# Forgetting attention: the reciprocals of the denominators multiply the head's result, as a row brought through DRAM, and v's remainders are made in one VectorE operation a block

## The chip, the cores and the metric

The kernel runs on one core of one Trainium2 chip. The metric is the device time of one execution in microseconds. Five engines work side by side, each through its own queue in order: TensorE (PE in the profile, its weight loads PEld), VectorE (DVE), ScalarE (ACT), GpSimd (POOL) and SyncE (SP), which here issues nearly all DMAs. The five meet through semaphores.

## The reference

One layer of a hybrid model in float32, for 512 tokens of width 1024: a feed-forward block, a mixing block with two branches (a chunked mLSTM and a forgetting attention), and a second feed-forward block, each with modulated normalisation and a residual. The change lies in the forgetting attention, 16 heads of width 64:

```python
def forgetting_attention(q, k, v, f_pre, q_g, k_g):
    ...
    F = jnp.moveaxis(jnp.cumsum(jax.nn.log_sigmoid(f_pre.astype(f32)), axis=1), 1, 2)
    ...
        logits = jnp.einsum('bhqd,bhkd->bhqk', q_blk, k).astype(f32) * scale + (F_blk[..., :, None] - F[..., None, :])
        logits = jnp.where(k_pos[None, :] <= q_pos[:, None], logits, -jnp.inf)
        p = jax.nn.softmax(logits, axis=-1)
        return jnp.einsum('bhqk,bhkd->bhqd', p.astype(v.dtype), v)
```

softmax divides each row of exponentials by its sum. The division may be made on the probabilities, before the product with v, or on that product, since the sum depends on the query alone.

## The kernel before

**Precision.** Every float32 product is made of rounded parts: an operand is split into a high part (the value as the matmul rounds it) and its remainder. `split` (L81) does it for weights: `raw` is loaded by SP (L78, three buffers), `wh` copied by ScalarE (L88), `wl` subtracted by VectorE (L89, four buffers each). `mm3` (L104) makes three matmuls of the four parts.

**The mixing stage.** After the gates and the mLSTM, `run` (L966 to L985) goes through 18 steps n. Step n calls `fox_s(n)`, `fox_o(n - 2)` and `fox_p(n - 1)`; between them stand pieces of a generator `fill`, which has the projections: `fox_qkv(g + 1)` makes q, k and v of the next group of four heads (chunks of weights, four token blocks each), and beside the last group `y_a` makes the mLSTM branch's output gate. `fox_t` makes the transposed q and k of a pair of heads.

**One head.** `fox_s` (L745): a row of decays `A0` is brought from DRAM (`A_d`) to all partitions by SP and masked by POOL into `Am` (L753). For each of four query blocks two matmuls (L761, L762) make logits in PSUM, VectorE adds the decays and takes the minimum of the negated logits (L764, L768, into `mn`), and ScalarE exponentiates (L772), with the sum of each row into `sm` (128 partitions x 4 blocks). `fox_p` (L775), one step later: the reciprocal of `sm` (L779), then four products on VectorE that scale the blocks of `S` (L782, 128 to 512 columns). Ten transposes on TensorE (L790) turn the blocks so that keys lie on partitions; each bank is split into `Ph` (ScalarE, L788) and its remainder `Pl` (VectorE, L789). `fox_o` (L806), one step after that: eight matmuls (L820) of `vt` with `Ph` and `Pl`. `vt` has the high part of v in 64 columns and its remainder in the next 64, so the two halves of the PSUM bank `po` are added: ScalarE copies one half to `tmp` (L823), VectorE adds the other and writes 64 rows of `yb` (L824).

**v.** In `fox_qkv`, `donev` (L697) adds the bias (VectorE, L699), and for each of two pairs of heads ScalarE copies the high part (L702) and POOL subtracts the remainder (L703), 128 columns each. POOL also scales q and k by their norms (L694), with the factors that VectorE's `rsqrt` made (L133 last).

**Order.** The kernel's text gives priorities and dependencies. The order in which each engine's queue has its instructions is made by the framework's scheduler when the kernel is built, from its own costs. On the chip each queue then keeps that order, and an instruction whose semaphore isn't there holds all behind it. PSUM has two pools of four banks, `pg` for projections (tile g) and `pt` for the rest (tile t). `yb` lies in the eight buffers that held x until it was stored to `x_d`; it is read only when the second branch is made (L999).

Of the kernel before, what the change touches and what calls it, by code (L numbers as in the profile page):

```python
# [11 lines left out]
F32 = mybir.dt.float32  # L12
F32R = mybir.dt.float32r
I32 = mybir.dt.int32
AF = mybir.ActivationFunctionType
# [5 lines left out]
P = 128  # L21
T = 512
NT = 4
# [18 lines left out]
P_OFF = (0, 128, 384, 768)  # L42
PT_OFF = (0, 768, 1152, 512)
MUL, ADD, SUB, MAX, MIN = ALU.mult, ALU.add, ALU.subtract, ALU.max, ALU.min


class Layer:
# [534 lines left out]
    def v_mlstm(self, half, ap, ip):  # L582
        nc, w = self.nc, self.A["w_mix"][0]
        bb = self.bias_bcast([(VM + half * 512, 512)], ip)
        vt = []
        for i in range(2):
            pair = [ap.tile([P, NT, 258], F32R, name=self.nm("vm"), tag="vm", bufs=6) for _ in range(2)]
            nc.scalar.activation(pair[0][:, :, 256:258], self.onz, AF.Copy)
            nc.scalar.activation(pair[1][:, :, 256:258], self.onz, AF.Copy, scale=0.0)
            vt.append(pair)  # L590
        def done(tb, ps):
            f = self.tmp(ip, "vf")
            nc.vector.tensor_tensor(f, ps, bb, op=ADD)
            for i in range(2):
                hi, lo = vt[i]
                s = slice(i * 256, (i + 1) * 256)
                nc.scalar.activation(hi[:, tb, 0:256], f[:, s], AF.Copy)
                nc.vector.tensor_tensor(lo[:, tb, 0:256], f[:, s], hi[:, tb, 0:256], op=SUB)
        def mk(ch):
            def make():  # L600
                wh, wl = self.w_mov(w, ch * 256, VM + half * 512)
                return wh, wl, 2 * ch, 2
            return make
        self.vt[2 * half:2 * half + 2] = vt
        yield from self.u_gemm_tokens([mk(c) for c in range(4)], 512, done)
# [60 lines left out]
    def fox_qkv(self, g, ip):  # L666

        nc, sp, w = self.nc, self.sp, self.A["w_mix"][0]
        o = g * 256
        bb = self.bias_bcast([(QF + o, 256), (KF + o, 256)], ip)  # L670
        tok = [ip.tile([P, 512], F32, name=self.nm("tk"), tag="tok", bufs=4) for _ in range(NT)]
        ss = sp.tile([P, NT, 8], F32, name=self.nm("fs"), tag="fs", bufs=2)
        def done(tb, ps):
            nc.vector.tensor_tensor(tok[tb], ps, bb, op=ADD)
            j = self.tmp(ip, "fj")
            nc.scalar.activation(j, tok[tb], AF.Square)
            nc.vector.tensor_reduce(ss[:, tb, :], j.rearrange("p (h d) -> p h d", h=8), AX.X, ADD)
        def mk(ch):
            def make():
                sh = [P, 2, 512]  # L680
                rows = w[ch * 256:(ch + 1) * 256]
                r = self.raw(sh, [(lambda t, i=i: t[:, :, i * 256:(i + 1) * 256],
                                   rows[:, c + o:c + o + 256].rearrange("(k p) n -> p k n", p=P))
                                  for i, c in enumerate((QF, KF))])
                wh, wl = self.split(r, sh)
                return wh, wl, 2 * ch, 2
            return make
        yield from self.u_gemm_tokens([mk(c) for c in range(4)], 512, done)
        v = sp.tile([P, NT * 8], F32, name=self.nm("fv"), tag="fv", bufs=2)
        nc.vector.tensor_scalar(v, ss.rearrange("p b h -> p (b h)"), 1.0 / 64, EPS, op0=MUL, op1=ADD)  # L690
        r = self.rsqrt(v, NT * 8)
        for tb in range(NT):
            t3 = tok[tb].rearrange("p (h d) -> p h d", h=8)
            nc.gpsimd.tensor_tensor(t3, t3, r[:, tb * 8:(tb + 1) * 8].unsqueeze(2).to_broadcast([P, 8, 64]), op=MUL)  # L694
        bv = self.bias_bcast([(VF + o, 256)], ip)
        vt = [ip.tile([P, NT, 2, P], F32R, name=self.nm("fvt"), tag="vm", bufs=6) for _ in range(2)]
        def donev(tb, ps):  # L697
            f = ip.tile([P, 256], F32, name=self.nm("vg"), tag="t2", bufs=3)
            nc.vector.tensor_tensor(f, ps[:, :256], bv[:, :256], op=ADD)  # L699
            for pr in range(2):  # L700
                f2 = f[:, pr * P:(pr + 1) * P].rearrange("p (h d) -> p h d", h=2)
                nc.scalar.activation(vt[pr][:, tb, :, 0:64], f2, AF.Copy)  # L702
                nc.gpsimd.tensor_tensor(vt[pr][:, tb, :, 64:P], f2, vt[pr][:, tb, :, 0:64], op=SUB)  # L703
        def mkv(ch):
            def make():
                sh = [P, 4, 256]
                r = self.raw(sh, [(lambda t: t, w[ch * 512:(ch + 1) * 512, VF + o:VF + o + 256]
                                   .rearrange("(k p) n -> p k n", p=P))])
                wh, wl = self.split(r, sh)
                return wh, wl, 4 * ch, 4  # L710
            return make
        self.fx[g] = (tok, vt)
        yield from self.u_gemm_tokens([mkv(c) for c in range(2)], 256, donev)
# [31 lines left out]
    def fox_s(self, h, ip):  # L745

        nc, sp = self.nc, self.sp
# [9 lines left out]
        for qb in range(NT):  # L757
# [12 lines left out]
                m = mn[:, qb, 1:2]  # L770
            ws = slice(o, o + (qb + 1) * P)
            nc.scalar.activation(S[:, ws], S[:, ws], AF.Exp, scale=-1.0, bias=m, accum_out=sm[:, qb:qb + 1])  # L772
        self.S[h] = (S, sm)

    def fox_p(self, h, ip):  # L775

        nc = self.nc
        S, sm = self.S[h]
        nc.vector.reciprocal(sm, sm)  # L779
        for qb in range(NT):  # L780
            ws = slice(P_OFF[qb], P_OFF[qb] + (qb + 1) * P)
            nc.vector.tensor_scalar(S[:, ws], S[:, ws], sm[:, qb:qb + 1], None, op0=MUL)  # L782
        Ph = ip.tile([P, 1408], F32R, name=self.nm("Ph"), tag="p6", bufs=5)
        Pl = ip.tile([P, 1408], F32R, name=self.nm("Pl"), tag="p6", bufs=5)
        nc.scalar.activation(Ph[:, 512:640], self.ident, AF.Copy, scale=0.0)
# [20 lines left out]
    def fox_o(self, h, ip):  # L806

        nc = self.nc
        g, i = h // 4, h % 4
        pr, hb = i // 2, (i % 2) * 64  # L810
        rows = slice(hb, hb + 64)
        vt = self.fx[g][1]
        Ph, Pl = self.S[h]
        po = self.tbank()
        blk = ((0, 0, 0), (1, 768, P), (2, 1152, 256), (3, 512, 256))
        n = 0
        for kb, o, q0 in blk:
            for Px in (Ph, Pl):
                n += 1
                nc.tensor.matmul(po[:, q0:], vt[pr][:, kb, i % 2, :], Px[:, o:o + T - q0], start=n == 1, stop=n == 8)  # L820
        tmp = self.tmp(ip, "yt")
        ot = slice(64 - hb, 128 - hb)
        nc.scalar.activation(tmp[rows, :], po[ot, :], AF.Copy)  # L823
        nc.vector.tensor_tensor(self.yb[2 * g + pr][rows, :], po[rows, :], tmp[rows, :], op=ADD)  # L824


    def y_a(self, m, ap, ip):
# [45 lines left out]
    def run(self):  # L873
        nc, tc, A = self.nc, self.tc, self.A
        gain = lambda r: self.colA[:, r:r + NK]
        self.x_d = self.dp.tile([T, D], F32, name="x_d")
        self.h_d = self.dp.tile([T, D], F32, name="h_d")

        self.ntmp, self.xn_tiles = 5, self.xn_start
        with tc.tile_pool(name="f1t", bufs=1) as tp:  # L880
# [175 lines left out]
```

## Time and profile before

| | |
|---|---|
| median of 3 runs | 1382.25 us |
| lowest, highest | 1380.84, 1384.68 us |
| the profiled execution | 1384.43 us |
| its span in the profile | 1382.7 us |
| mean granted TensorE clock | 0.993 |
| instructions | 17469 |
| DMA, mean over the span | 127 GB/s |

The page gives busy time by engine, the chain of work that ended last and the costliest groups. A busy TensorE is not one at its peak, and the engines' shares are means over stages that differ: the mixing stage's attention lies between 560 and 800 us. There, windows (busy time of each engine in a stretch), the timeline (instructions in order of time, with the idle time before one and what ended it, in brackets) and the waits (who waited for whom, total, times, longest) say more than the page. In a group's row stand the line, the engine, the operation, result and operands, the shapes and the count, then total and mean time, then the engine's idle time before such an instruction.

### The profile page before, as it was taken

How to read it: one execution, taken by the hardware profiler on the slowest of the kernel's cores; microseconds unless marked ns; L12 is line 12 of the kernel's file. 1: busy time of each engine (PE TensorE's matmuls, PEld its weight loads, DVE VectorE, ACT ScalarE, POOL GpSimd, SP SyncE). 2: the span in 40 equal slices, each digit the busy share in tenths (PEclk: the TensorE clock that was granted, in tenths of full speed). 3: DMA queues.
4: the chain of work that ended last, by engine and by line, in shares of the span. 5: the costliest groups of instructions: out<-in, count | busy, mean ns of one | idle time of the engine just before them, and what ended most of it. 6: DMA issues, size and time to landing. Idle time of an engine off the chain costs nothing.

```text
span 1382.7 us, 17469 instructions
## 1 busy us (share of the span) xinstructions
PE 1349.1 (98%) x6570; PEld 1128.7 (82%) x6570; DVE 797.0 (58%) x1439; ACT 554.4 (40%) x940; POOL 131.0 (9%) x151
## 2 busy tenths in 40 slices
PE   6999999999999999999999999999999999999998
PEld 5788887887888888788787888888888888888887
DVE  7865666656467788888798542444473333332232
ACT  4442333323237654667567542422353232232120
POOL 4200000000011101331431100011010000000000
PEclk9999999999999999999999999999999999999999
DMA  9665556665533433432334233533313333333330
GB/s 290 193 204 178 183 183 206 212 207 194 178 80 107 131 92 110 130 92 78 95 82 119 69 99 101 159 92 106 107 53 116 106 92 96 103 92 96 110 122 31
DMA packets 212392, 176.02 MB, mean 127 GB/s; under 512 B 10386, under 2 KB 182066, under 8 KB 212308
## 3 DMA queue, kind: packets, MB, share of 16 engines
q1 hardware_dynamic: 211828, 174.83, 42.0%
q8 instruction: 52, 0.85, 0.3%
q14 instruction: 32, 0.26, 0.1%
q0 software_dynamic: 416, 0.06, 0.0%
q10 hardware_dynamic: 64, 0.02, 0.0%
HBM read 168.51 MB, written 6.36 MB: 126 GB/s over the span
## 4 chain that ended last, share of the span: by engine, by line
PE 84%; DVE 9%; ACT 3%; issue 2%; SPq 1%; DMA 1%; POOL 1%; DVEq 0%; ACTq 0%; POOLq 0%
PE g L108 22%; PE g L106 22%; PE g L107 22%; PE t L106 4%; PE t L108 4%; PE t L107 4%; DVE wl L89 2%; PE t L820 1%; PE t L790 1%; ACT wh L88 1%; DMA ar<-in_w_ada_dram 1%; DVE ac L444 1%; PE t L761 1%; DVE S L782 1%; PE t L762 1%
## 5 line engine op out<-in xcount | busy, mean ns | idle before, releaser
L89 DVE TENSOR_TENSOR wl<-raw,wh 128x1024 fp32r<-128x1024 f32 x214 | 273.6, 1279 | 309.2 <-ACT wh L88 289.8
L88 ACT ACTIVATE wh<-raw 128x1024 fp32r<-128x1024 f32 (+1 forms) x221 | 231.7, 1053 | 516.7 <-PE g L107 192.4
L108 PE MATMUL g<-uh,wl 128*128 128x512 f32 (+2 forms) x984 | 369.8, 377 | 1.7 <-DVE wl L89 1.7
L106 PE MATMUL g<-uh,wh 128*128 128x512 f32 (+2 forms) x984 | 370.9, 378 | 0.0
L107 PE MATMUL g<-ul,wh 128*128 128x512 f32 (+2 forms) x984 | 370.3, 377 | 0.0
L108 PEld LDWEIGHTS g<-uh,wl 128*128 128x128 f32 (+1 forms) x984 | 185.0, 188 | 36.4 <-DVE wl L89 2.6
L106 PEld LDWEIGHTS g<-uh,wh 128*128 128x128 f32 (+1 forms) x984 | 185.2, 188 | 34.1 <-ACT wh L88 0.6
L107 PEld LDWEIGHTS g<-ul,wh 128*128 128x128 f32 (+1 forms) x984 | 185.3, 188 | 33.6
L106 PE MATMUL g<-wh,uh 128*128 128x512 f32 (+1 forms) x320 | 113.4, 354 | 0.0
L107 PE MATMUL g<-wl,uh 128*128 128x512 f32 (+1 forms) x320 | 112.2, 351 | 0.0
L108 PE MATMUL g<-wh,ul 128*128 128x512 f32 (+1 forms) x320 | 112.1, 350 | 0.0
L325 DVE TENSOR_TENSOR sl<-g,sl 128x512 f32<-128x512 f32 (+1 forms) x45 | 30.0, 666 | 86.7 <-PE g L108 86.5
L284 DVE SCALAR_TENSOR_TENSOR acc<-raw,ccol,acc 128x1024 f32<-128x1024 f32 x49 | 62.8, 1282 | 16.2 <-DMA raw<-in_w_ada_dram 15.6
L106 PE MATMUL g<-wh,hh 128*128 128x512 f32 x176 | 69.3, 394 | 0.0
L108 PE MATMUL g<-wh,hl 128*128 128x512 f32 x176 | 69.2, 393 | 0.0
L106 PE MATMUL t<-wh,hh 128*128 128x512 f32 x176 | 69.1, 393 | 0.0
L107 PE MATMUL t<-wl,hh 128*128 128x512 f32 x176 | 69.1, 392 | 0.0
L107 PE MATMUL g<-wl,hh 128*128 128x512 f32 x176 | 69.1, 392 | 0.0
L108 PE MATMUL t<-wh,hl 128*128 128x512 f32 x176 | 69.1, 392 | 0.0
L108 PEld LDWEIGHTS g<-wh,ul 128*128 128x128 f32 x320 | 61.0, 191 | 7.8
L106 PEld LDWEIGHTS g<-wh,uh 128*128 128x128 f32 x320 | 61.2, 191 | 7.1
L107 PEld LDWEIGHTS g<-wl,uh 128*128 128x128 f32 x320 | 61.2, 191 | 7.0
(264 smaller groups left out, 1930.0 us busy)
## 6 DMA issues: line engine op xcount, KB each, us to landing
raw<-in_ffn_w_in_dram SPq DMA_DIRECT2D x82, 512.0 KB, 4.0
raw<-in_w_ada_dram SPq DMA_DIRECT2D x56, 512.0 KB, 3.4
raw<-in_w_mix_dram SPq DMA_DIRECT2D x48, 512.0 KB, 4.1
raw<-in_ffn_w_out_dram SPq DMA_DIRECT2D x44, 512.0 KB, 4.2
raw<-in_w_mix_dram SPq DMA_DIRECT2D x32, 256.0 KB, 2.9
ar<-in_w_ada_dram SPq DMA_DIRECT2D x28, 256.0 KB, 6.0
A<-A_d SPq DMA_DIRECT2D x16, 256.0 KB, 4.0
raw<-in_w_branch_a_dram SPq DMA_DIRECT2D x8, 512.0 KB, 4.2
```

Of the source, the lines that this page charges most:

```text
L88: nc.scalar.activation(hi, src, AF.Copy)
L89: (eng or nc.vector).tensor_tensor(lo, src, hi, op=SUB)
L106: mm(ps, lh, rh, start=start, stop=False)
L107: mm(ps, lh, rl, start=False, stop=False)
L108: self.last_mm = mm(ps, ll, rh, start=False, stop=stop)
L284: nc.vector.scalar_tensor_tensor(acc, r, self.ccol[:, k:k + 1], acc, op0=MUL, op1=ADD)
L325: nc.vector.tensor_tensor(s[:, :w], ps_b[:, c0:c1], s[:, :w], op=MUL)
L444: nc.vector.scalar_tensor_tensor(a, r[:, i], cc, a, op0=MUL, op1=ADD)
L761: nc.tensor.matmul(ps[:, :w], q[:, s], k[:, :w], start=True, stop=False)
L762: nc.tensor.matmul(ps[:, :w], q[:, s], kl[:, :w], start=False, stop=True)
L782: nc.vector.tensor_scalar(S[:, ws], S[:, ws], sm[:, qb:qb + 1], None, op0=MUL)
L790: tr = lambda b, c, qb, kb: nc.tensor.transpose(b[:, c:c + P], S[:, P_OFF[qb] + kb * P:P_OFF[qb] + (kb + 1) * P], self.ident)
```

## The change

Four things are changed.

- The scaling of `S` in `fox_p` is left out; `Ph` and `Pl` hold exponentials that are not normalised.
- The reciprocal of `sm` is made at the end of `fox_s`. Two DMAs on SP follow it: one writes the 128 x 4 reciprocals to a DRAM tile of the head, `r_d[h]`, as a row of 512 in the order of the tokens; the other reads that row into 64 partitions of `yb`, where the head's result will stand.
- `fox_o` adds the halves into `tmp` and then multiplies `tmp` with what stands in `yb`, in one more VectorE operation of 64 x 512.
- `vt` is one tile for four heads instead of two for a pair each, so that ScalarE copies the 256 columns of a block in one operation; the remainders are made by one VectorE operation instead of two on POOL. The mLSTM's v tiles, which share the buffers, are allocated in pairs accordingly.

```diff
--- before.py
+++ after.py
@@ -584,7 +584,8 @@
         bb = self.bias_bcast([(VM + half * 512, 512)], ip)
         vt = []
         for i in range(2):
-            pair = [ap.tile([P, NT, 258], F32R, name=self.nm("vm"), tag="vm", bufs=6) for _ in range(2)]
+            t = ap.tile([P, 2, NT, 258], F32R, name=self.nm("vm"), tag="vm", bufs=3)
+            pair = t[:, 0], t[:, 1]
             nc.scalar.activation(pair[0][:, :, 256:258], self.onz, AF.Copy)
             nc.scalar.activation(pair[1][:, :, 256:258], self.onz, AF.Copy, scale=0.0)
             vt.append(pair)
@@ -693,14 +694,13 @@
             t3 = tok[tb].rearrange("p (h d) -> p h d", h=8)
             nc.gpsimd.tensor_tensor(t3, t3, r[:, tb * 8:(tb + 1) * 8].unsqueeze(2).to_broadcast([P, 8, 64]), op=MUL)
         bv = self.bias_bcast([(VF + o, 256)], ip)
-        vt = [ip.tile([P, NT, 2, P], F32R, name=self.nm("fvt"), tag="vm", bufs=6) for _ in range(2)]
+        vt = ip.tile([P, NT, 4, P], F32R, name=self.nm("fvt"), tag="vm", bufs=3)
         def donev(tb, ps):
             f = ip.tile([P, 256], F32, name=self.nm("vg"), tag="t2", bufs=3)
             nc.vector.tensor_tensor(f, ps[:, :256], bv[:, :256], op=ADD)
-            for pr in range(2):
-                f2 = f[:, pr * P:(pr + 1) * P].rearrange("p (h d) -> p h d", h=2)
-                nc.scalar.activation(vt[pr][:, tb, :, 0:64], f2, AF.Copy)
-                nc.gpsimd.tensor_tensor(vt[pr][:, tb, :, 64:P], f2, vt[pr][:, tb, :, 0:64], op=SUB)
+            f4 = f.rearrange("p (h d) -> p h d", h=4)
+            nc.scalar.activation(vt[:, tb, :, 0:64], f4, AF.Copy)
+            nc.vector.tensor_tensor(vt[:, tb, :, 64:P], f4, vt[:, tb, :, 0:64], op=SUB)
         def mkv(ch):
             def make():
                 sh = [P, 4, 256]
@@ -770,16 +770,18 @@
                 m = mn[:, qb, 1:2]
             ws = slice(o, o + (qb + 1) * P)
             nc.scalar.activation(S[:, ws], S[:, ws], AF.Exp, scale=-1.0, bias=m, accum_out=sm[:, qb:qb + 1])
-        self.S[h] = (S, sm)
+
+        nc.vector.reciprocal(sm, sm)
+        nc.sync.dma_start(self.r_d[h].rearrange("b p -> p b"), sm)
+        rows = slice(h % 2 * 64, h % 2 * 64 + 64)
+        nc.sync.dma_start(self.yb[h // 2][rows, :].rearrange("p (b t) -> p b t", b=NT),
+                          self.r_d[h][None, :, :].to_broadcast([64, NT, P]))
+        self.S[h] = S
 
     def fox_p(self, h, ip):
 
         nc = self.nc
-        S, sm = self.S[h]
-        nc.vector.reciprocal(sm, sm)
-        for qb in range(NT):
-            ws = slice(P_OFF[qb], P_OFF[qb] + (qb + 1) * P)
-            nc.vector.tensor_scalar(S[:, ws], S[:, ws], sm[:, qb:qb + 1], None, op0=MUL)
+        S = self.S[h]
         Ph = ip.tile([P, 1408], F32R, name=self.nm("Ph"), tag="p6", bufs=5)
         Pl = ip.tile([P, 1408], F32R, name=self.nm("Pl"), tag="p6", bufs=5)
         nc.scalar.activation(Ph[:, 512:640], self.ident, AF.Copy, scale=0.0)
@@ -817,11 +819,13 @@
         for kb, o, q0 in blk:
             for Px in (Ph, Pl):
                 n += 1
-                nc.tensor.matmul(po[:, q0:], vt[pr][:, kb, i % 2, :], Px[:, o:o + T - q0], start=n == 1, stop=n == 8)
+                nc.tensor.matmul(po[:, q0:], vt[:, kb, i, :], Px[:, o:o + T - q0], start=n == 1, stop=n == 8)
         tmp = self.tmp(ip, "yt")
         ot = slice(64 - hb, 128 - hb)
         nc.scalar.activation(tmp[rows, :], po[ot, :], AF.Copy)
-        nc.vector.tensor_tensor(self.yb[2 * g + pr][rows, :], po[rows, :], tmp[rows, :], op=ADD)
+        nc.vector.tensor_tensor(tmp[rows, :], po[rows, :], tmp[rows, :], op=ADD)
+        y = self.yb[2 * g + pr][rows, :]
+        nc.vector.tensor_tensor(y, tmp[rows, :], y, op=MUL)
 
 
     def y_a(self, m, ap, ip):
@@ -875,6 +879,7 @@
         gain = lambda r: self.colA[:, r:r + NK]
         self.x_d = self.dp.tile([T, D], F32, name="x_d")
         self.h_d = self.dp.tile([T, D], F32, name="h_d")
+        self.r_d = [self.dp.tile([NT, P], F32, name=f"r_d{h}") for h in range(16)]
 
         self.ntmp, self.xn_tiles = 5, self.xn_start
         with tc.tile_pool(name="f1t", bufs=1) as tp:
```

## Prediction

> **What bounds the kernel now.** First the page: TensorE is busy for nearly the whole span, so a change that leaves its matmuls alone can only win back its idle time and its slow time. The change touches the forgetting attention, 560 to 800 us, so I cut that stretch by windows (columns: length, then busy time and count of PE, weight loads, DVE, ACT, POOL; granted clock; DMA share; GB/s).
>
> ```profile
> PE 1349.1 (98%) x6570; PEld 1128.7 (82%) x6570; DVE 797.0 (58%) x1439; ACT 554.4 (40%) x940; POOL 131.0 (9%) x151
> ```
>
> ```profile
> 600.00:620.00 20.00, 17.64 (x118) 15.21 (x117) 16.63 (x42) 10.42 (x25) 10.82 (x13) 1.00 0.34 96
> 660.00:680.00 20.00, 16.70 (x88) 14.37 (x87) 14.22 (x30) 11.73 (x27) 7.24 (x10) 0.83 0.31 91
> 720.00:740.00 20.00, 16.34 (x80) 13.12 (x79) 14.25 (x30) 14.28 (x29) 4.01 (x6) 0.91 0.52 131
> 560.00:800.00 240.00, 228.83 (x1312) 196.26 (x1311) 193.97 (x537) 157.11 (x355) 62.77 (x63) 0.98 0.33 93
> ```
>
> TensorE idles 240 - 228.8 = 11.2 us in the stage, and 9.3 of them lie in three windows (2.36, 3.30, 3.66): the places where one group of four heads hands over to the next. In two of them the clock also falls; 20 x (1 - 0.83) = 3.4 and 20 x (1 - 0.91) = 1.8 us of full-speed work are lost there. So the most that can be won is about 11.2 + 5.2 = 16 us. Who ends these gaps is in TensorE's waits and timeline:
>
> ```profile
> PE t L733 <- POOL tk L694: 1.8, 2, 1.1
> ```
>
> ```profile
> 668.99 0.69 PE L790 MATMUL t<-ident,S 128*128 128x128 f32 x2 [3.31 <-DVE Pl L789]
> 669.90 0.63 PE L107 MATMUL g<-wl,uh 128*128 128x512 f32 x1
> 670.33 0.63 PE L108 MATMUL g<-wh,ul 128*128 128x512 f32 x1
> 726.62 1.09 PE L790 MATMUL t<-ident,S 128*128 128x128 f32 x4 [3.52 <-DVE fq L740]
> ```
>
> After the 3.31 us gap one matmul of 512 columns follows the other by 0.43 us: that is the half clock. The waits of 1.1 us and less in the first window left the clock at 1.00. VectorE ends two gaps itself and feeds the third (POOL's L694 starts when VectorE's r is done). VectorE ahead of the second gap, and POOL beside it:
>
> ```profile
> 655.52 1.99 DVE L89 TENSOR_TENSOR wl<-raw,wh 128x1024 fp32r<-128x1024 f32 x1
> 657.54 0.69 DVE L824 TENSOR_TENSOR yb<-t,yt 64x512 f32<-64x512 f32 x1
> 658.60 3.32 DVE L782 TENSOR_SCALAR S<-S,sm 128x128 f32<-128x128 f32 x3
> 662.18 0.77 DVE L782 TENSOR_SCALAR S<-S,sm 128x512 f32<-128x512 f32 x1
> 662.87 1.48 DVE L89 TENSOR_TENSOR wl<-raw,wh 128x1024 fp32r<-128x1024 f32 x1
> 666.21 1.23 DVE L89 TENSOR_TENSOR wl<-raw,wh 128x1024 fp32r<-128x1024 f32 x1 [1.20 <-ACT wh L88]
> ```
>
> ```profile
> 655.29 5.12 POOL L694 TENSOR_TENSOR tk<-tk,rq 128x512 f32<-128x512 f32 x4 [7.31 <-DVE rq L133]
> 661.67 3.00 POOL L703 TENSOR_TENSOR fvt<-vg,fvt 128x128 fp32r<-128x128 f32 x4
> ```
>
> VectorE works through here almost without a pause, and the scalings L782 that the change removes stand in the middle. Three of them take 3.32 us while POOL computes L694, and one wl takes 1.99 us beside L694, 1.48 beside L703, and 1.23 with POOL between two operations.
>
> **The change part by part.** 1. **The scalings go.** What they take ahead of each gap is one answer of the windows, cut to L782 (busy, count):
>
> ```profile
> 599.90:604.90 5.00, 2.57 (x7) 1.00 0.41 124
> 650.00:668.20 18.20, 5.61 (x8) 1.00 0.30 88
> 707.00:725.00 18.00, 5.63 (x8) 1.00 0.33 82
> ```
>
> Over the stage they are the four groups of 16 below, 9.3 + 8.7 + 7.2 + 5.8 = 31.0 us. The transposes L790 then follow the exponentials alone.
>
> ```profile
> L824 DVE TENSOR_TENSOR yb<-t,yt 64x512 f32<-64x512 f32 x16 | 10.9, 682 | 1.3 <-ACT yt L823 1.0
> L782 DVE TENSOR_SCALAR S<-S,sm 128x512 f32<-128x512 f32 x16 | 9.3, 580 | 0.0
> L782 DVE TENSOR_SCALAR S<-S,sm 128x384 f32<-128x384 f32 x16 | 8.7, 543 | 0.0
> L782 DVE TENSOR_SCALAR S<-S,sm 128x256 f32<-128x256 f32 x16 | 7.2, 448 | 0.0
> L789 DVE TENSOR_TENSOR Pl<-t,Ph 128x256 fp32r<-128x256 f32 x16 | 6.6, 412 | 0.0
> L782 DVE TENSOR_SCALAR S<-S,sm 128x128 f32<-128x128 f32 x16 | 5.8, 360 | 0.2
> ```
>
> 2. **The product with the row** is one more operation on 64x512 a head, behind L824. By L824's 0.68 us it is 16 x 0.68 = 10.9 us. L824 reads one operand from PSUM and the product none; the bound below is the same, the bound above is a wl's 1.99 for twice the columns.
>
> 3. **v's remainders** move from POOL to VectorE, 16 operations of 128x256; by the row of Pl at that size 0.41 us each, 6.6 us. POOL loses L703, and ScalarE does one copy where it did two. In each of the two large stretches there are four. They wait for ScalarE's copy; VectorE has the next bias add or a wl to do meanwhile, so I take nothing for that.
>
> VectorE's balance is -31.0 + 10.9 + 6.6 = -13.5 us. What counts is the balance ahead of the gaps. First: -2.57 + 0.69 = -1.9; second and third: -5.6 + 0.7 + 4 x 0.41 = -3.3 each. Successive operations overlap by about 0.08 us in the timeline (the busy sums count that twice), so I take -1.4, -2.7 and -2.7, and 0.3 more for each of the latter two because no L703 runs beside wl any longer (1.48 against 1.23). The gaps of TensorE become 2.36 - 1.4 = 1.0, 3.3 - 3.0 = 0.3 and 3.66 - 3.0 = 0.7. Gaps of that size left the clock alone in the first window, so the slow clock goes too: 3.4 + 1.8, less 0.5 that lay in the gaps. Sum: 1.4 + 3.0 + 3.0 + 4.7 = 12.1 us. What is late next is ScalarE, which already ends VectorE's pause of 1.20 us above.
>
> 4. **The reciprocal moves** from the head of fox_p, one head later, to the end of fox_s. There it must wait for the head's last exponential:
>
> ```profile
> 644.25 0.08 DVE L768 DVE_READ_ACCUMULATOR2_ANT mn<- 128x1 f32 x1
> ```
>
> ```profile
> 644.88 0.71 ACT L772 ACTIVATE S<-S,mn 128x512 f32<-128x512 f32 x1
> 645.49 0.18 ACT L772 ACTIVATION_READ_ACCUMULATOR S<-S,mn 128x1 f32 x1
> ```
>
> From the last minimum (644.33) to the sum (645.67) are 1.34 us. Behind the reciprocal on VectorE stand the next wl, tk and fs, for which TensorE waits only near the gaps. The order of each engine's queue is chosen by the framework's scheduler, which can put other work into those 1.34 us, as it did in this row. Bounds: nothing, and 1.34 for each of two heads ahead of each gap, 3 x 2 x 1.34 = 8.0 us. I take 2.5, nearer to nothing, because in the profile the reciprocal had such work around it at every head.
>
> 5. **Two DMAs a head on SP's queue**, 32 in all. The write scatters 512 elements of 4 bytes; the read spreads one 2 KB row to 64 partitions. The read cannot be issued before the write has landed, and SP issues in order, so weight loads behind it are held. The trace has no such write. Nearest rows: the store of h_d, 1.9 us to landing, and gbias, some elements of 4 bytes each on POOL's queue; issuing 1024 small pieces of rawg took SP up to 0.93 us:
>
> ```profile
> h_d<-hn SPq DMA_DIRECT2D x12, 128.0 KB, 1.9
> ```
>
> ```profile
> DMA to landing us min/median/max: 4.7/5.1/5.6
> ```
>
> ```profile
> L506 SPq DMA_DIRECT2D rawg<-in_w_mix_dram x3: 383/709/932, 410.9 to 412.1; - x3
> ```
>
> So SP is held 0.7 + 1.9 to 0.7 + 5.1 us from the reciprocal on. What covers it are the three raw buffers: a load goes out when VectorE has finished a wl, and is used three chunks later.
>
> ```profile
> 657.57 7.23 SPq L78 DMA_DIRECT2D raw<-in_w_mix_dram  x2
> ```
>
> ```profile
> 677.88 1.04 ACT L88 ACTIVATE wh<-raw 128x1024 fp32r<-128x1024 f32 x1
> ```
>
> ```profile
> raw<-in_w_mix_dram SPq DMA_DIRECT2D x16, 512.0 KB, 4.3
> ```
>
> The first of these two loads, sent when the wl of 655.52 was done, lands at 657.6 + 4.3 = 661.9 and is read at 677.9: 16 us of cover against a hold of 2.6 to 5.8. I cost the DMAs at nothing. Without the cover each would cost its hold, 16 x 5.8 = 93 us. The row is needed two heads later, some 240 / 16 x 2 = 30 us, so the product does not wait for it.
>
> Sum: 12.1 - 2.5 = 9.6 us off the profiled execution, 1384.43 us (span 1382.7, 1.7 around it): 1374.8. That run stood 2.2 us above the median of the three runs, 1382.25, so from the median: 1372.7, rounded to 1373.
>
> **The rivals.** **A, the reciprocal's wait eats the gain.** If it stands in VectorE's queue right behind the last minimum, the upper bound holds: 2.7 us are lost ahead of each gap, the gaps stay at 2.4, 3.0 and 3.4 us, and the slow clock with them. About 1 us is won: 1381. For it: no operation can pass a waiting one on its engine. Against: the scheduler interleaves freely (644.25 row). Chance 0.12.
>
> **B, the new operations are held by POOL.** The product and the remainders read both operands from SBUF, like wl, which lost 1.99 - 1.23 = 0.76 us beside L694. Five such operations stand ahead of each of the last two gaps: 5 x 0.76 = 3.8 us, more than the 3.0 won there. Only the first gap's 1.4 us would be left: 1381. Against it: L694 runs for 5.1 us and cannot meet all five, and the scalings that go met it too (3.32 us for three). Chance 0.11. The Trainium skill (SBUF — State Buffer, "SBUF: two separate sides") says that a VectorE operation with two SBUF inputs and a GpSimd operation that reads SBUF lock each other out for a whole instruction; the wl rows agree with it in kind, though 0.76 us is less than one L694.
>
> **C, the loads of weights come late (slower).** SP reaches the write before its reciprocal is ready and waits there as it now waits for a buffer:
>
> ```profile
> SPq L750 <- DVE mn L764: 58.6, 13, 9.5
> ```
>
> The longest of those waits is 9.5 us; with 0.9 of issue, 5.1 to landing and 0.3 for the read's issue that is 15.8, just under the 16 us of cover. From 16 us on TensorE starves. A hold of 20 us in one head of each group costs 4 x 4 us, and gaps over 3.3 us bring the slow clock again, about 4 x 3 us; with the 9.6 won, 1382 + 28 - 9.6 = 1401. For it: SP is in order, and the read waits for a landing. Against: loads are sent when VectorE frees a buffer, and the reciprocal is in the same VectorE queue. Chance 0.17. The Trainium skill (DMA: Bandwidth & Descriptors, "Rules for kernel authors") warns that a transfer whose last dimension is not contiguous becomes one descriptor for each element and should be rearranged, 512 of them here; no run here shows their price.
>
> **How the numbers follow.** The forecast with its variants (a gap closed more or less) has 0.60, A and B together 0.23, C 0.17. About 0.3%, 4.1 us, is what a measurement can tell from no change. Low end: all 16 us of the stage, 1366, less 2 for the scatter of runs: 1364. High end: A and B at 1381 and the near half of C, a hold just over its cover: 1388. Faster 0.60, same 0.23, slower 0.17.
>
> **What would show it.** Right: PE's idle time in 560 to 800 falls from 11.2 to 4 us or less with the clock at 1.00; VectorE's busy time there falls by 10 to 15 us; "raw" stays absent from ACT's waits. A shows as VectorE waiting for ACT's S ahead of the reciprocal, over 6 us in sum; B as products and remainders of 1.2 us and more; C as wh waiting for DMA raw. I am wrong if the gaps are ended by something else than VectorE's work, so that they stay while VectorE's time falls.

## The result, and the profile after

The changed kernel takes 1399.45 us (median of 4 runs, 1397.35 to 1401.68), the kernel before 1382.03 in the same series: a ratio of 1.0125 [1.0105, 1.0145]. Every ratio here is to the kernel before in the same series, with its 95% interval in brackets. The forecast was 1373 with a range of 1364 to 1388. The sign was wrong, and the time lies outside the range.

The line numbers after the change are those of the new file: L695 is POOL's scaling of q and k (L694 before), L703 the v remainders, L774 the reciprocal, L775 the write to `r_d`, L777 the read into `yb`, L828 the product with the row. The first view is the page of the changed kernel, busy time by engine:

```profile
PE 1353.9 (97%) x6570; PEld 1131.4 (81%) x6570; DVE 795.5 (57%) x1407; ACT 554.3 (40%) x924; POOL 109.9 (8%) x119
```

The 6570 matmuls are the same, but TensorE needs 4.8 us more for them (1349.1 before); its mean clock is 0.989 where it was 0.993. VectorE's busy time has hardly fallen, 795.5 us against 797.0. Next the windows of the changed kernel, with the columns of the prediction:

```profile
600.00:620.00 20.00, 14.35 (x106) 13.18 (x105) 14.27 (x41) 7.70 (x19) 7.97 (x6) 0.87 0.32 74
660.00:680.00 20.00, 15.21 (x111) 13.86 (x110) 17.30 (x45) 8.75 (x22) 8.43 (x6) 0.90 0.36 82
720.00:740.00 20.00, 16.93 (x117) 15.48 (x116) 17.91 (x45) 9.75 (x22) 7.64 (x6) 0.94 0.34 80
560.00:816.00 256.00, 234.67 (x1310) 200.17 (x1311) 189.96 (x496) 156.92 (x342) 45.06 (x36) 0.95 0.44 96
```

The stage has become 16 us longer for the same matmuls (1312 and 1310 in these windows). TensorE idles 256 - 234.7 = 21.3 us in it instead of 11.2, and the clock over the stage is 0.95 instead of 0.98. VectorE was to lose 10 to 15 us here; it has 190.0 where it had 194.0. The handovers between groups of four heads are still the worst places. What ends the waits there is another engine than before; these are the waits of TensorE, and the longest of SP's queue (total, times, longest):

```profile
PE t L733 <- POOL tk L695: 13.4, 12, 2.9
PE t L761 <- DVE mn L764: 3.4, 1, 3.4
```

```profile
SPq L777 <- DMA r_d<-sm: 133.2, 16, 10.7
```

SP stands at every one of the 16 reads, 8.3 us in the mean, until the write ahead of it has landed. The view of DMA issues gives the landing of the 2 KB write as 8.7 us, more than that of a 512 KB load of weights, and the decay rows as later than before the change; the last line is the kernel before:

```profile
raw<-in_w_mix_dram SPq DMA_DIRECT2D x16, 512.0 KB, 5.2
A<-A_d SPq DMA_DIRECT2D x15, 256.0 KB, 5.9
...
yb<-r_d SPq DMA_DIRECT2D x16, 128.0 KB, 3.1
r_d<-sm SPq DMA_DIRECT2D x16, 2.0 KB, 8.7
```

```profile
A<-A_d SPq DMA_DIRECT2D x16, 256.0 KB, 4.0
```

How this reaches TensorE can be read in three timelines of the changed kernel around the second handover, SP's first (start, duration of the issue, what is issued):

```profile
657.20 0.37 SPq L775 DMA_DIRECT2D r_d<-sm  x1
665.98 0.45 SPq L777 DMA_DIRECT2D yb<-r_d  x1
666.52 0.54 SPq L562 DMA_DIRECT2D bb<-in_b_mix_dram  x1
667.16 0.38 SPq L750 DMA_DIRECT2D A<-A_d  x1
```

```profile
672.26 1.54 POOL L753 TENSOR_TENSOR Am<-A,maskF 128x512 f32<-128x512 f32 x1 [9.92 <-DMA A<-A_d]
673.76 5.63 POOL L695 TENSOR_TENSOR tk<-tk,rq 128x512 f32<-128x512 f32 x4
```

```profile
675.04 0.33 PE L733 MATMUL t<-ident,tk 128*128 128x128 f32 x1 [1.60 <-POOL tk L695]
...
679.44 0.90 PE L733 MATMUL t<-ident,tk 128*128 128x128 f32 x3 [1.51 <-POOL tk L695]
```

The write goes out at 657.20; the read can only follow at 665.98, 8.8 us later. The bias rows and the decay row stand behind the read and go out at 666.52 and 667.16. POOL has waited 9.92 us for the decay row when it starts the mask at 672.26. Its four scalings of q and k stand behind the mask in its queue and start at 673.76, 3.2 us after VectorE had their factors ready (670.59), and TensorE's transposes of q and k wait for them one by one. The weights, of which the prediction had asked whether they have cover, are not in this chain: ScalarE's copies `wh` wait for TensorE alone in this stage.

### The profile page after: what moved, and what is told of

Read it like the earlier page. It is cut to its first block, busy times and chain, and to the rows that moved or that the text cites. A ratio compares the mean times of both kernels' runs of the same rounds, so it can differ in the third digit from the quotient of the medians.

```text
span 1398.9 us, 17459 instructions
## 1 busy us (share of the span) xinstructions
PE 1353.9 (97%) x6570; PEld 1131.4 (81%) x6570; DVE 795.5 (57%) x1407; ACT 554.3 (40%) x924; POOL 109.9 (8%) x119
## 4 chain that ended last, share of the span: by engine, by line
PE 81%; DVE 9%; DMA 3%; ACT 2%; issue 2%; POOL 2%; SPq 1%; POOLq 0%; DVEq 0%; ACTq 0%
PE g L108 22%; PE g L106 22%; PE g L107 22%; PE t L108 4%; PE t L107 4%; PE t L106 4%; DMA A<-A_d 2%; POOL tk L695 1%; DVE wl L89 1%; PE t L822 1%; PE g L490 1%; PE t L792 1%; DVE ac L444 1%; DVE fs L678 1%; DVE tk L675 1%
```

## The experiments

The first theory, **HOLD**, is the chain above: SP stands at the read, and the small loads behind it come late. Its rival, **ORDER**, is that the scheduler made other queue orders for the changed kernel (POOL has all masks of a group ahead of its scalings), and that these cost the time. Four runs tell them apart.

**The read one head later.** The read of head h - 1 is put on SP behind the write of head h; the orders of the other engines are unchanged.

```diff
-        nc.sync.dma_start(self.r_d[h]..., sm)
-        nc.sync.dma_start(self.yb[h // 2]..., self.r_d[h]...)
+        w = nc.sync.dma_start(self.r_d[h]..., sm)
+        if h:
+            with self.tc.issue_after(w.ins):
+                self.row_in(h - 1)
+        if h == 15:
+            self.row_in(h)
```

> The read of a head's row is put behind the next head's write on SP's queue; the queues of the other four engines keep the changed kernel's order. Theory HOLD (SP stands at the read until the write, 8.7 us, has landed, and the decay rows A0 behind it come late): the 133 us that SP waits at the read fall below 15, TensorE's 13.4 us of waiting for POOL's tk fall below 4, and the time falls to 1370 to 1380. Rival ORDER (the new order on POOL and VectorE costs by itself): TensorE goes on waiting for tk and the time stays above 1392.

Measured: 1392.19 us, ratio 1.0065 [1.0045, 1.0085], far above HOLD's range and just at the bound of ORDER. SP's and TensorE's waits in this run:

```profile
SPq L785 <- DMA r_d<-sm: 22.9, 7, 7.5
```

```profile
PE t L733 <- POOL tk L695: 5.5, 7, 0.9
PE t L761 <- DVE mn L764: 5.3, 1, 5.3
```

With the stand of SP reduced from 133.2 to 22.9 us (below 15 was expected), TensorE's waits for POOL's scalings fall from 13.4 to 5.5 (below 4 was expected). Half of the loss is gone, and half stays, with one gap of 5.3 us at head 2.

**Neither DMA.** Both are left out, and the last product multiplies the head's result with itself.

```diff
-        nc.sync.dma_start(self.r_d[h]..., sm)
-        nc.sync.dma_start(self.yb[h // 2]..., self.r_d[h]...)
...
-        nc.vector.tensor_tensor(y, tmp[rows, :], y, op=MUL)
+        nc.vector.tensor_tensor(y, tmp[rows, :], tmp[rows, :], op=MUL)
```

> Both DMAs are left out and the last product multiplies tmp with itself, so the result is not normalised; every engine but SP has the changed kernel's order. HOLD: as e1_read_late within 3 us, 1368 to 1380, which is what the arithmetic of the change is worth without its transfers. ORDER: above 1392.

Measured: 1383.35 us, ratio 1.0001 [0.9992, 1.0011], 3 us above HOLD's range. The two DMAs cost the whole loss. With the same orders the time is that of the kernel before, so ORDER falls as its cause. Nor do the masks hold the scalings here: in this run's trace POOL starts them at 606.46, 660.03 and 715.15, each time when VectorE's factors `rq` come. But the arithmetic of the change, which was to win some 10 us, wins nothing even without them; that is taken up below.

**The v part alone**, on the kernel before, and **the row part alone**, with v as before (each has one half of the diff shown with the change):

> Only v's part of the change: one tile for four heads, one ScalarE copy and one VectorE remainder a block; the scalings stay as before. POOL's queue has the order of the changed kernel but for one place. HOLD: SP is not held, so 1376 to 1386, near the kernel before (VectorE has 6.6 us more work, POOL 20 us less). ORDER: 1390 or more.

> Only the row's part of the change: no scalings, reciprocal in the score step, write and read on SP, product at the end; v as before with its remainders on POOL. HOLD: SP is held 120 us or more and the time is slow like the changed kernel's, 1392 to 1404. ORDER (v's move to VectorE and the new place of Am on POOL is what costs): 1385 or less.

Measured: the v part 1379.56 us, ratio 0.9983 [0.9974, 0.9992]; the row part 1402.22 us, ratio 1.0143 [1.0126, 1.016], with SP waiting for `r_d` 16 times, up to 10.5 us. The loss belongs to the row.

What kept half of the loss in the first run? Heads 0 and 1 write only 3 us apart, and head 0's read still stood there. The next runs were to settle it.

**The read behind the next head's write, for head 0 too.** Head 0's read goes behind the write of head 2.

```diff
+    def row_in(self, h):
+        rows = slice(h % 2 * 64, h % 2 * 64 + 64)
+        with self.tc.issue_after(self.wr[min(h + 1, 15) if h else 2].ins):
+            self.nc.sync.dma_start(self.yb[h // 2]..., self.r_d[h]...)
...
                 if n >= 2:
+                    self.row_in(n - 2)
                     self.fox_o(n - 2, ip)
```

> The change with the read of a head's row put on SP behind the write of the next head (as in the run with the read one head later), and head 0's read behind the write of head 2, so that heads 0 and 1, whose writes are 3 us apart, hold nothing up either. The orders of PE and POOL are those of the change; on VectorE one product (head 0's) comes later. HOLD (SP standing at the read is the cost, the writes and reads themselves are free): 1383 to 1386 us, near the run without the two DMAs (1383.4); SP's wait for r_d<-sm at most 5 us in sum (133.2 in the change, 22.9 with the reads one head later), the 5.5 us gap at head 2's first score matmul gone. TRAFFIC (512 four-byte elements a write slow the loads beside them: A<-A_d 5.9 us to land against 4.0 in the kernel before): 1390 us or more, with A still above 5 us and VectorE waiting for POOL's Am although SP waits nowhere.

Measured: 1399.73 us, ratio 1.0126 [1.0111, 1.0141]. HOLD is refuted as the whole cause. At heads 0 and 1 SP waits for no write, and the gap at head 2 is still there, 6.2 us. (Over the stage SP's waits for `r_d` sum to 14.8 us, where 5 was expected.) SP and POOL in this run:

```profile
574.84 0.40 SPq L775 DMA_DIRECT2D r_d<-sm  x1
575.75 0.32 SPq L750 DMA_DIRECT2D A<-A_d  x1
```

```profile
589.47 1.26 POOL L753 TENSOR_TENSOR Am<-A,maskF 128x512 f32<-128x512 f32 x1 [15.71 <-DMA A<-A_d]
```

The decay row goes out right behind the write, at 575.75, and POOL has it at 589.47: 13.7 us. These are the same places in the run without DMAs:

```profile
576.35 0.91 SPq L750 DMA_DIRECT2D A<-A_d  x2
```

```profile
580.49 2.57 POOL L753 TENSOR_TENSOR Am<-A,maskF 128x512 f32<-128x512 f32 x2 [6.70 <-DMA A<-A_d]
```

There it takes 4.1 us. In the run with the moved reads a second gap came from the move itself: VectorE waits in the product for the row.

```profile
596.92 1.61 SPq L781 DMA_DIRECT2D yb<-r_d  x2
```

```profile
607.41 0.68 DVE L831 TENSOR_TENSOR yb<-yt,yb 64x512 f32<-64x512 f32 x1 [6.49 <-DMA yb<-r_d]
```

The two reads went out at 596.92, half a microsecond behind a write, and their rows were there some 10 us later; in the changed kernel, where SP had waited for the landing first, it took 3.1 us. So in both places what is issued right behind one of these writes comes late, though SP waits at no read there. I call this **STALL**.

**The write as four rows of 512 bytes.** TensorE turns the 128 x 4 denominators, ScalarE copies them, and the DMA writes contiguous rows; the read stands right behind it as in the change.

```diff
-        nc.sync.dma_start(self.r_d[h].rearrange("b p -> p b"), sm)
+        b = self.tbank()
+        nc.tensor.transpose(b[0:NT, 0:P], sm, self.ident)
+        rw = self.tmp(ip, "rw")[0:NT, 0:P]
+        nc.scalar.activation(rw, b[0:NT, 0:P], AF.Copy)
+        nc.sync.dma_start(self.r_d[h], rw)
```

> The change with the denominators turned on TensorE (one 128x4 transpose a head, copied by ScalarE) so that the write is four rows of 512 bytes and not 512 elements of four bytes; the read right behind it as in the change. The orders of PE, ACT and POOL are not those of the change. If the landing of 512 elements is the price (8.7 us): r_d lands in 2 to 3.5 us, SP's wait at the read falls from 10.7 us to some 3 to 5, and the time to 1386 to 1392 us. If any write that a read follows at once holds SP that long: landing and wait stay above 8 us and the time at 1396 to 1402.

Measured: 1387.23 us, ratio 1.0036 [1.0023, 1.005]. SP's wait and the first write and read of this run:

```profile
SPq L781 <- DMA r_d<-rw: 10.9, 11, 2.6
```

```profile
575.64 0.30 SPq L779 DMA_DIRECT2D r_d<-rw  x1
...
577.11 0.51 SPq L781 DMA_DIRECT2D yb<-r_d  x1
```

The same 2 KB, written as 4 pieces instead of 512, let the read go 1.5 us later instead of 8.8, and 12 of the 17 us are gone. The landing is the price of the pieces, not of a write as such, nor of a read that follows it. How much of the 12 us this is isn't separated: the orders of TensorE, ScalarE and POOL are others in this run.

**The write alone** separates the writes from SP's stand at the reads: no read is issued.

```diff
-        rows = slice(h % 2 * 64, h % 2 * 64 + 64)
-        nc.sync.dma_start(self.yb[h // 2]..., self.r_d[h]...)
...
-        nc.vector.tensor_tensor(y, tmp[rows, :], y, op=MUL)
+        nc.vector.tensor_tensor(y, tmp[rows, :], tmp[rows, :], op=MUL)
```

> The change without the read of the rows: the 16 writes r_d<-sm stay, the last product multiplies the head's result with itself, so that the result isn't normalised. Nothing on SP waits for a write any more; the orders of PE, ACT and POOL are those of the change. HOLD (only SP standing at the read costs): 1382 to 1386 us, as without both DMAs (1383.4). STALL (512 four-byte elements keep the DMA engines from everything behind them for some 9 us, whoever waits: in e6_read_behind_next a decay row issued at 575.75 us landed 13.7 us later, with SP free): 1388 to 1394 us, with the gap of 5 to 6 us at head 2's first score matmul still there and decay rows that land some 13 us after their issue behind the writes of heads 0 and 1; the boundaries at 610, 670 and 730 us as without the DMAs.

Measured: 1390.52 us, ratio 1.0048 [1.0033, 1.0063], as STALL has it. The gap at head 2 is 3.3 us, as in the changed kernel (3.4) and less than the 5 to 6 expected. The decay row of head 2 goes out at 574.79, and POOL has it 10.8 us later, a little less than the 13 expected; in the changed kernel itself it goes out at 574.73 and POOL has it at 585.65. This run:

```profile
574.79 0.32 SPq L750 DMA_DIRECT2D A<-A_d  x1
575.16 0.43 SPq L78 DMA_DIRECT2D raw<-in_w_mix_dram  x1
```

```profile
585.59 1.26 POOL L753 TENSOR_TENSOR Am<-A,maskF 128x512 f32<-128x512 f32 x1 [12.51 <-DMA A<-A_d]
```

How busy the DMA engines were (in tenths) and what they moved, in 40 slices of 1 us from 570 us on in this run:

```profile
DMA  6499500221007799999922995998710073249496
GB/s 154 82 297 326 100 0 0 12 16 8 8 8 35 108 196 323 244 51 32 9 2 28 113 122 74 101 165 240 198 26 8 3 79 49 45 160 95 116 304 102
```

From 575 to 582 us, with a decay row and weights on order since 574.79 and 575.16, they move at most 16 GB/s. The run without DMAs, with the same stores of `h_d` just ahead, moves 183 to 252 GB/s from 576 to 580. SP is not free in this run either:

```profile
576.90 1.65 SPq L750 DMA_DIRECT2D A<-A_d  x1
579.18 4.06 SPq L78 DMA_DIRECT2D raw<-in_w_mix_dram  x2
```

These issues take 0.34 us, and 0.90 for two, without the DMAs. In the trace the long ones wait for a semaphore that an earlier store of `h_d` still has in use, though they read nothing of it; so a late landing holds SP in this way too.

**The write issued by ScalarE** asks whether another queue avoids this; it is the run before with `nc.scalar` in place of `nc.sync` at the write.

> e10_write_only (1390.5 us) with the 16 writes issued by ScalarE and not by SP; no read, the product multiplies the head's result with itself, so the result isn't normalised. The order of TensorE's matmuls differs in 18 rows near head 2. If the element writes keep the DMA engines themselves (STALL): the decay row of head 2 still lands 9 us or more after its issue, the engines are still nearly full at under 40 GB/s for some 5 us behind a pair of writes, and the time is 1387 to 1394 us. If only the loads of the same queue stand behind the elements: the decay rows land within 6 us and the time is 1382 to 1386 us, as without the DMAs, or up to 3 more for ScalarE's wait for the reciprocal ahead of the issue.

Measured: 1389.22 us, ratio 1.0053 [1.0037, 1.007]. The same slices of this run:

```profile
DMA  0171899699933897973005913488999300232676
GB/s 0 43 180 39 159 300 162 20 36 38 22 16 20 95 129 151 145 160 125 0 0 12 38 11 34 56 173 202 232 281 262 40 0 3 47 81 17 160 106 200
```

After the write that ScalarE issues at 573.37, the engines again move under 40 GB/s, from 577 to 583, and the time is as STALL has it. So another queue does not avoid the low rate. It isn't the same in all: up to 581 the engines are recorded as 0.6 busy and more, where they were under 0.3 in the run before. The Trainium skill (DMA: Bandwidth & Descriptors, "Issuing engines are not separate DMA queues") says that DMAs started by different engines run on the same 16 DMA engines and interleave; this agrees. What stood in this run was ScalarE, which issued its second write only at 584.25, and SP, which waited 7.9 us ahead of a decay row for the first write's semaphore. The landing of head 2's decay row can't be read here: the profile puts the end of POOL's wait for it to VectorE.

**Contiguous write and late read together** (the two edits shown above):

> e7_contiguous_write (1387.2 us) with the read of a head's row put on SP behind the write of the next head. The orders of PE, DVE and POOL are those of e7. SP's wait at the read, 10.9 us in sum there, goes to under 2. If what is left over the run without DMAs (1383.4) is still SP standing: 1384 to 1386 us. If it is the added transposes and copies (16 of each) with the order that they force: 1386.5 to 1388 us, as e7.

Measured: 1387.73 us, ratio 1.0032 [1.0022, 1.0042], no gain over the contiguous write alone. SP no longer waits for `r_d`, so that stand is not what remains over the run without DMAs. The added transposes take 4.3 us of TensorE (16 of 270 ns, as modelled in the profile), which is the size of what remains. That they are its cause isn't shown: the orders differ, the DMAs are still there, and SP now waits 28.5 us in sum for ScalarE's copies ahead of the writes.

The second question is why the arithmetic wins nothing. **CHAIN**: the handovers are now ended by the norm's factors and POOL's four scalings, 4.9 us. **LOAD**: VectorE is late there as before, whatever POOL does. Two of the four scalings are given to VectorE, first on the run with the moved reads:

```diff
-            nc.gpsimd.tensor_tensor(t3, t3, r[...]..., op=MUL)
+            (nc.vector if tb % 2 else nc.gpsimd).tensor_tensor(t3, t3, r[...]..., op=MUL)
```

> The run e6_read_behind_next with two of the four q/k scalings of a head group (128x512 each) on VectorE in place of POOL. Tests why the change's arithmetic wins nothing even without its DMAs (1383.4 against 1382.7 before). CHAIN (the boundary of a head group is now ended by rq and then POOL's four scalings, 4.9 us, for which TensorE waits some 1.8 us at each of three boundaries): TensorE's waits for tk fall from 5.3 us to 2 or less, 1378 to 1382 us, 3 to 6 under e6. LOAD (VectorE itself is what the boundaries wait for, whatever POOL does): no gain, 0 to +4 against e6, with other waits for VectorE in the place of tk.

Measured: 1398.13 us, ratio 1.0116 [1.0098, 1.0135], 1.6 us under its base: unclear, since the two DMA gaps are in it. TensorE's waits for `tk` do go, from 5.1 to 0.2 us. To this, v's remainders of the first group were given back to POOL, since TensorE waits 2.4 us for VectorE's `hn` where they stand ahead of it (0.9 in the kernel before):

```diff
-            nc.vector.tensor_tensor(vt[:, tb, :, 64:P], f4, vt[:, tb, :, 0:64], op=SUB)
+            (nc.vector if g else nc.gpsimd).tensor_tensor(vt[:, tb, :, 64:P], f4, vt[:, tb, :, 0:64], op=SUB)
```

> e8_tk_shared with the v remainders of the first head group alone back on POOL, one operation a block; the others stay on VectorE. Tests that the 2.6 us gap ahead of the last mLSTM matmuls (TensorE waits 2.4 us for VectorE's hn; 0.9 in the kernel before) comes from these remainders standing ahead of hn on VectorE. If so: the wait is 1 us or less, the slow clock behind it goes too, and the time is 2 to 3.5 us under e8, 1375 to 1380 us, below the kernel before and below the v part alone (1379.6). If the gap is ended by something else: within 1 us of e8. The order of TensorE's matmuls around 550 to 580 us differs a little from e8's.

> The v part alone (e2_v_alone, 1379.6 us) with the v remainders of the first head group back on POOL, one operation a block. In e9 the same edit took TensorE's wait for hn from 1.9 to 0.6 us, but the time stayed (1398.5 against 1398.1), where gaps of 4 and 7 us follow that other DMAs end. If that wait (2.4 us in e2, and the slow clock behind it) is worth its length: 1376 to 1378 us. If the time is given back at the next waits, for tk and Pl behind it: within 1 us of e2, 1379 to 1380.5.

Measured: 1398.49 us (ratio 1.0118 [1.0099, 1.0137]) on that base, and 1380.02 us (ratio 0.9973 [0.9963, 0.9984]) on the v part alone. The wait for `hn` did fall, from 1.9 to 0.6 us and from 2.4 to 1.1. The time did not fall with it on the first base; on the second the ratio is 0.001 lower, with intervals that overlap.

Then without DMAs. First **the reciprocal back in `fox_p`**, where the kernel before has it:

```diff
-        nc.vector.reciprocal(sm, sm)
-        self.S[h] = S
+        self.S[h] = S, sm
...
-        S = self.S[h]
+        S, sm = self.S[h]
+        nc.vector.reciprocal(sm, sm)
```

> The run without the two DMAs (e5_no_dmas, 1383.4 us) with the reciprocal back at the start of fox_p, where the kernel before has it; the product still multiplies the head's result with itself, so the result isn't normalised. PE's and POOL's orders are unchanged. My step 4 priced the reciprocal's wait for ScalarE at 2.5 us, and the rival at up to 21. If that wait is what eats the arithmetic's gain: 1379 to 1381 us, and VectorE's waits for ScalarE's S at the reciprocal (7.7 us in sum in the change) gone. If the gain was never there, since the boundaries are ended by rq and POOL's tk: 1382.5 to 1385, as e5.

Measured: 1379.57 us, ratio 0.9969 [0.9959, 0.9979]. The time is the one forecast for a wait that goes, but the wait did not go. VectorE at the reciprocal, in the changed kernel and in this run:

```profile
DVE sm L774 <- ACT S L772: 7.7, 11, 0.9
```

```profile
DVE sm L780 <- ACT S L772: 6.2, 8, 0.9
```

And on this, the shared scalings:

> e14_recip_late_no_dmas (1379.6 us; ratio 0.9969 to the kernel before) with two of the four q/k scalings of a head group on VectorE in place of POOL; the order of PE is unchanged. The product still multiplies the head's result with itself, so the result isn't normalised. CHAIN (with the scalings of the scores gone, the boundary of a head group is ended by rq and then POOL's four operations of 1.2 us): TensorE's wait for tk, 5.0 us in sum, goes to 1 or less, nothing takes its place, and the slow clock behind the boundaries goes too: 1373 to 1376 us, ratio 0.992 to 0.995. LOAD (VectorE itself is late at the boundary, so that the next of its products is waited for, as Pl and fq were in e8, 2.2 us at a boundary): 1378.5 to 1381 us, ratio 0.996 to 0.999.

Measured: 1381.23 us, ratio 0.9998 [0.9987, 1.0009]: no gain, just above LOAD's range and far from CHAIN's. In the trace TensorE's order differs from the base's in some 50 of 6570 matmuls. TensorE's main waits in the two runs, from 560 to 800 us, the base first:

```profile
PE t L733 <- POOL tk L695: 5.0, 6, 0.9
PE t L106 <- DVE hn L655: 2.4, 1, 2.4
PE t L761 <- DVE ya L843: 1.3, 1, 1.3
PE t L788 <- DVE fq L740: 0.7, 1, 0.7
```

```profile
PE t L788 <- DVE Pl L787: 3.9, 2, 2.2
PE t L788 <- DVE fq L740: 2.7, 2, 2.0
PE t L106 <- DVE hn L655: 1.9, 1, 1.9
PE t L761 <- DVE ya L843: 1.3, 2, 1.1
PE t L761 <- DVE Pl L787: 1.0, 3, 0.5
PE t L733 <- DVE tk L695: 0.4, 2, 0.2
```

The waits for `tk` go from 5.0 to 0.4 us, and waits for `Pl` and `fq`, products of VectorE, take their place. The rows sum to 9.4 us in the first run and 11.2 in the second. CHAIN named the engine that ends the waits rightly, but ending them moved them.

## Why the prediction was wrong

**Step 5 failed: "I cost the DMAs at nothing."** It went wrong in two places.

*The landing.* The write's landing was taken from the store of h_d and the load of gbias, 1.9 to 5.1 us. It is 8.7. Neither row has a write of single elements, and the prediction had itself cited the Trainium skill (DMA: Bandwidth & Descriptors, "Rules for kernel authors") that such a transfer becomes one descriptor for each element, here 512 a head. It gave the rule no price. The run with 4 pieces in place of 512 now shows one: the read goes out 1.5 us behind the write, not 8.8.

*The cover.* The 16 us of cover are those of the weights, and they held: SP's stands of up to 10.7 us never made `wh` wait. But the decay rows and the bias rows stand in the same queue, and their cover was not looked up. POOL waits for a decay row, and behind it in POOL's queue stand the scalings on which TensorE waits at a handover. The step asked for the cover of the largest transfer behind the wait, where the smallest cover counts.

By the ratios, the arithmetic alone is 1.0001, with the writes 1.0048, with the reads behind them 1.0125. At 1382 us the writes cost 6.5 us, through the late loads behind them and what waits for these, and the reads, with SP's stand at them, another 10.6. The split depends on where the reads are: one head later, 1.0065, most of that second part goes (not in the run with the moved reads, 1.0126, where VectorE waits for a late row), and with the contiguous write most of both.

**Rival C** gave 1401 us (its own terms add up to 1400.4) with a chance of 0.17, and the time is 1399.5. The sign and the resource were right (SP in order, a read that waits for a landing). Its mechanism was not: the weights never came late, and the hold lies well under its decision point of 16 us. That the figures agree is chance.

**Step 1** was right: the scalings went, 31.0 us of VectorE.

**Steps 2 and 3** were too small. This is the changed kernel, the product and the remainders:

```profile
L828 DVE TENSOR_TENSOR yb<-yt,yb 64x512 f32<-64x512 f32 x16 | 14.2, 886 | 0.4
L703 DVE TENSOR_TENSOR fvt<-vg,fvt 128x256 fp32r<-128x256 f32 x16 | 11.6, 748 | 1.6 <-ACT fvt L702 1.6
```

They were put at 10.9 and 6.6 us. The balance is -31.0 + 14.2 + 11.6 = -5.2 us, not -13.5. The sizes were taken from rows that read one operand from PSUM, where the new operations read both from SBUF, and most of the difference is rival B. (In the trace of the kernel before, nine of the 16 L824 ran beside POOL and none took over 698 ns, so that row couldn't show it.) First the remainders of the changed kernel as shortest, median and longest; then their group's row in the run with half of POOL's scalings moved away:

```profile
L703 DVE TENSOR_TENSOR fvt<-vg,fvt x16: 411/426/1393, 554.4 to 737.5; 128x256 fp32r<-128x256 f32 x16
```

```profile
L703 DVE TENSOR_TENSOR fvt<-vg,fvt 128x256 fp32r<-128x256 f32 x16 | 6.5, 422 | 0.8 <-ACT fvt L702 0.6
```

Most take what the step said, but some up to 1393 ns. In the trace of the changed kernel each of the six remainders over 1.1 us runs beside one of POOL's scalings, and each of the four products over 1.1 us beside a mask or a scaling; with POOL idle none takes more than 426 and 690 ns. With half of the scalings moved away the mean of the remainders is 422 (715 in the run that this was done on). This agrees with the rule of the Trainium skill that the rival cited (SBUF — State Buffer, "SBUF: two separate sides"). But B did not decide: that run has the cheap remainders and no gain in time.

**The 12.1 us** of the closed gaps did not come. The prediction subtracted the removed work from the gaps as if nothing else ended them; this step failed too. Its last sentence named the way in which this fails. In the run with the reciprocal back and no DMAs, the gaps of 3.3 and 3.5 us ahead of the transposes L790 are gone but for one of 0.7, and six waits for `tk`, 0.9 us at most, stand at the handovers in their place. The v part alone wins 0.17%, and the row's arithmetic adds nothing clear to it. What takes its place is read from the waits, and shown once, by the shared scalings; what else would have to go for a gain is open. (Two slips in the working decide nothing: at 0.08 us an operation, with eight operations out and five in, the overlap at the second and third gap is about 0.24 us and not 0.6, and by rival A's own 2.7 us the first gap becomes 3.7 us and not 2.4.)

**Step 4**, the reciprocal's wait, stood at 2.5 us. The changed kernel shows VectorE waiting there 11 times, 7.7 us in sum, 0.9 at most. That is over the 6 us which the prediction had named as the sign of rival A, so the sign came. What it costs in time is open. The runs with the reciprocal in the two places have 1.0001 and 0.9969, with intervals that don't meet, but 6.2 of the 7.7 us of waiting are still there in the second, TensorE's order differs in some places, and the run with the shared scalings, which has the reciprocal back too, is again at 0.9998. I don't count it as shown.

Two kernels beat the kernel before: the v part alone at 0.9983 [0.9974, 0.9992], and the same with the first group's remainders on POOL at 0.9973 [0.9963, 0.9984]. Of the change, only this half is worth keeping.

## What to carry to other kernels

Price a transfer by the number of its pieces and by what is issued behind it, and not by its bytes alone. Before costing a wait in an in-order queue at nothing, list every load that stands behind it and take the one with the least cover, together with what is queued behind that load's reader. And where several operations of one engine feed a handover, taking some of its work away can move the wait to the next operand, as here: look for that operand before the gap is counted as won.

## What was not expected of the hardware

Writing 512 elements of 4 bytes kept later transfers back, though 2 KB are little: a decay row issued behind it took 10.8 to 13.7 us to arrive where it took 4.1, and for some 7 us the DMA engines moved at most 16 GB/s with work on order. In the run with the write alone the elements' own packets are recorded as 9 ns each and as done by 575 us, where the low rate begins, so the profile shows that the loads stand still but not what they stand at. Issuing the write from ScalarE's queue left the rate under 40 GB/s for 6 us. What holds the engines was not settled.
